# One starting address modulo 512 bytes for the matmul operands, and a gap of 8 columns between two token streams

## The chip, the cores and the metric

The kernel runs on one core of one Trainium2 chip. The metric is the device time of one execution in microseconds (us); lower is better. The kernel before has a median of 1493.14 us over three runs (1492.9 to 1493.96).

## The reference

Two streams of tokens pass through two layers of width 1024: 512 latent tokens and 256 context tokens. Each layer is a token mixer and a ConvFFN, each behind an RMS norm with a modulation (scale, shift, gate) made from a condition vector.

```python
def conv_mixers(h, ...):              # layer 0, both streams
    g_b, g_c, u_a, v_b, gate_b = split(h @ w_in)          # 1024 -> 2560
    y_a = g_b * dwconv3(g_c * u_a)
    u = dwconv31(v_b * sigmoid(gate_b)) + bias
    return concat([y_a, silu(layernorm(u))]) @ w_out      # 1024 -> 1024
def windowed_gqa(h, hc, ...):         # layer 1: 16 heads, 4 key heads, +-128 tokens and all context
    ...
def conv_ffn(h, w_up, conv, w_down):  # both layers; layer 1 for the latent tokens only
    a, g = split(dwconv3(h @ w_up))                       # 1024 -> 2 x 2816
    return (silu(g) * a) @ w_down                         # 2816 -> 1024
```

The output is the latent stream after a last RMS norm, in float32.

## The kernel before

Channels lie on the 128 partitions and tokens along the free dimension. One tile holds 128 channels of both streams side by side: columns 0 to 511 are latent tokens, then a gap of zeros, then 256 context columns from column `C0`; the whole width is `T` (770 columns, lines 27 and 28). The gap lets one elementwise instruction, and one three-tap convolution, run over both streams at once.

**Products.** Float32 precision comes from three products of split operands. Weights are loaded by a DMA into `wraw` and split into `whi` and `wlo` (ACT L158, DVE L159); activations are split the same way into pairs `h` (high and low), `gh` and `gl`, `oh` and `ol`. For each 128-channel tile k of the contraction, `mm3` (L176 to L178) issues three matmuls: `wlo` with the high part, `whi` with the low part, `whi` with the high part. The weights are the stationary operand, 128 columns of 4 bytes, so 512 bytes of each partition; the tokens are the moving operand. `wide_gemm` (L187) runs the 512 latent columns over all k first, then the 256 context columns: 24 matmuls of 512 columns and 24 of 256 for one output tile with eight k.

```python
        for k in range(len(rhs)) if ks is None else ks:                       # L183
            xh, xl = rhs[k]
            self.mm3(out, w, k, xh[:, lo:hi], xl[:, lo:hi], k == first, k == last)
```

**Stages in order.** (1) First norm and the first part of the modulation, with three output tiles of `w_in` alongside. (2) The rest of the 20 tiles of `w_in`; DVE runs the 31-tap convolution between (L577, `tap`), and 12 half pieces of the modulation go between as small products (L225). (3) `w_out`, 8 tiles, half of them held until the LayerNorm of the wide convolution is through. (4) FFN of layer 0: 44 up tiles with eight k, then 22 k for each of 8 down tiles in five groups (`up`, `down`). (5) Keys (2 tiles), queries (8 tiles) and values of layer 1. (6) Attention, with transposes and products in float32, and the output projection `w_o` in two halves of 256 tokens. (7) FFN of layer 1 for 512 latent tokens: the first 6 up tiles and the last group of down products in two halves of 256 columns, the others 512 columns wide. (8) The last norm, transposed out.

**Order.** The order on each engine comes from the program and from a planner that lists the instructions with a time model; `issue_after` ties a few steps to others. Every weight load is issued from SP's queue into a ring of three `wraw` tiles; `whi` and `wlo` are rings of three in the pool `wts`, and some weights go to spare tiles of the current phase instead.

**Where tiles lie.** Each pool is a stretch of SBUF. Constants, `x`, weights and temporaries lie at the low end, the tiles of a phase after them; the pools called `right` (`act` with the tiles `h`, `core`, and the phase `ffn1`) end at the top. A tile takes a multiple of 32 bytes in each partition. At the bottom lies a scratch of 16384 bytes for DMA descriptors, which this kernel's DMAs (all from SP) don't use. A tile that reuses the room of an older one waits for the older one's last use.

```python
C0 = SEQ + 2                                                                  # L27
T = C0 + CTX                                                                  # L28
    self.x = [self.cst.tile([P, T], F32, name=f"x{k}") for k in range(KT)]    # L118
    hi, lo = into or (self.wts.tile([P, 1024], F32R, name=t, tag=t, bufs=3) for t in ("whi", "wlo"))   # L165
    return [tuple(self.act.tile([P, n], F32R, name="h", ...) for c in "hl") for k in range(KT)]        # L328
    gh = self.ph.tile([P, width], F32R, name="gh", tag=f"gh{j}")              # L604
```

From these sizes the starts modulo 512 bytes follow. A tile of `T` columns is 3080 bytes, takes 3104, and 3104 = 6 x 512 + 32, so of a row of such tiles each starts 32 bytes further on. The weights' rings start at 224. The 16 tiles `h` of layer 0 (high and low of k = 0, then of k = 1, and so on) start at 480, 0, 32, 64, ... up to 448, so the high part of k = 4 starts at 224. A context column block starts 514 x 4 = 2056 = 4 x 512 + 8 bytes into its tile. In the FFN of layer 1 the tiles `h` are 512 columns wide and all start at 352; `gh` and `gl` all start at 480, and the weights of the down products lie at 480 (spare tiles of the phase, two of each three) or at 224 (the ring). `oh` and `ol` start at 352.

Of the kernel before, what the change touches and what calls it, by code (L numbers as in the profile page):

```python
# [26 lines left out]
C0 = SEQ + 2  # L27
T = C0 + CTX  # L28
FF = 2816
# [28 lines left out]
class Kern:  # L58
# [38 lines left out]
    def gap(self, slot):  # L97
        """Zeros between the two streams of an accumulator that is as wide as both."""
        self.nc.vector.memset(slot[:, SEQ:C0], 0.0)

# [10 lines left out]
    def setup(self):  # L111
# [5 lines left out]
        self.par = self.cst.tile([P, NPAR], F32, name="par")  # L117
# [12 lines left out]
        # modulation: [ch, layer, chunk*8 + tile, condition]  # L130
        self.mod = self.cst.tile([P, 2, 48, 2], F32, name="mod")
        # gain * (1 + scale): [ch, norm, tile, condition]
# [8 lines left out]
    def turn(self, slots):  # L141
        """A new round of accumulators."""
        self.slots, self.slot_i = slots, 0

    def taken(self):
        """An accumulator, out of the round, and the others in the order in which they come up."""
        s = self.slot()
        i = self.slot_i % len(self.slots)
        return s, (self.slots[i:] + self.slots[:i])[:-1]
# [6 lines left out]
    def split(self, src, hi, lo):  # L156
        """hi + lo = src, each of at most twelve significant bits."""
# [3 lines left out]
    def weights(self, dram, n=1024, into=None):  # L161
        """The two parts of a stretch of weights."""
# [6 lines left out]
    def spare(self, i, n=1024, tags=("whi", "wlo")):  # L169
        """Room for more weights in the current phase."""  # L170
# [9 lines left out]
    def gemm(self, out, w, rhs, lo, hi, ks=None, ends=None):  # L180
        """out = w.T @ rhs[lo:hi], or the tiles ks of a sum from the first to the last of ends."""
# [9 lines left out]
    def places(self, segs):  # L191
        """New accumulators for stretches of tokens."""
# [6 lines left out]
    def side_by_side(self, slots, rhs, segs):  # L199
        """Products with the weights at hand, all of them with one tile of rhs before the next."""  # L200
# [13 lines left out]
    def mod_piece(self, l, lo, hi, at, dram, acc, tr, room):  # L214
        """512 columns of w_mod, as four column tiles of the array: two feature tiles in each half of lo..hi; in two steps."""
# [25 lines left out]
    def mod_rows(self, l, j0, n, conds):  # L241
        """n feature tiles from j0 of w_mod transposed, to be done one after the other."""
# [31 lines left out]
    def square_in(self, k, lo, hi, sq=None):  # L274
        """Adds x[k]**2 to the sum over channel tiles."""
# [9 lines left out]
    def inverse(self, ss, chunks, ones2, comp, eng):  # L285
        """1 / sqrt(mean + EPS) of each token, tokens on the partitions; one column for each chunk of them."""
# [7 lines left out]
        # a first guess from the exponent's bits, then Newton's steps  # L294
# [8 lines left out]
    def rstd(self, ss, segs, ones2, slot, eng=None, pool=None, project=None):  # L303
        """1 / sqrt(mean + EPS) for each token, the same in every partition, in PSUM."""
# [21 lines left out]

    def new_h(self, n=T):
        return [tuple(self.act.tile([P, n], F32R, name="h", tag=f"h{c}{k}") for c in "hl") for k in range(KT)]  # L328

    def mod_in(self, h, k, r, n, l, shift, segs):  # L330
        """h[k] = rmsnorm(x[k]) * gain + shift, in two parts."""
# [5 lines left out]
        for s0, s1 in segs:  # L337
# [4 lines left out]
            if k < 2:  # L342
                # the shorter way for the tiles that are waited for
# [20 lines left out]
    def conv3(self, acc, u, w, n):  # L364
        """acc = three taps over u (zero between the streams)."""
# [5 lines left out]
    def project(self, w, n, rhs, segs, l, chunk, ms=range(KT), lead=0, late=0, few=(), room={}):  # L371
        """x += gate * (w.T @ rhs). The late feature tiles take the last tokens in a second step, with the weights they
        still hold; those in the lead wait for the last of rhs side by side. The last of the steps stops
        after each number in few of its tiles. room: where weights go."""
# [36 lines left out]
    def start(self, ph):  # L411
        """First norm and modulation; value and gate of the wide convolution's first channels alongside."""
# [35 lines left out]
    def layer0_input(self, h, sl):  # L448
        """Value and gate of the wide convolution's channels, then the narrow convolution; the wide one's taps between."""
# [16 lines left out]
    def gates(self):  # L466
        """The rest of the modulation, half a piece at a time."""
# [8 lines left out]
    def layer0_output(self, y):  # L476
        """Output projection: the narrow convolution's channels while the wide one's norm is under way, then the others."""
# [30 lines left out]
    def tokens_in_turn(self, segs, project, norm, first, early=1, room=()):  # L508
        """Projects one stretch of tokens after the other; the norm of each hides behind the next products."""
        self.pre = [self.weights(w) for w in first[:early]]  # L510
        next(project)
        self.h = self.new_h(segs[-1][1])
# [9 lines left out]
    def spread(self, seg, project=None):  # L522
        """1 / rms of a stretch of tokens in SBUF, a step of other work alongside."""
# [8 lines left out]
    def tap(self, n):  # L532
        """n taps of the wide convolution, channel tiles in turn so that none waits for the one before it."""
        for _ in range(n):
# [3 lines left out]
            # the first two tiles first, and those that have the most to go  # L538
# [8 lines left out]
    def tile_in(self, m, h, segs):  # L547
        """One tile of the input projection, its weights made ready one tile ahead."""
# [8 lines left out]
    def glu(self, j, v, g):  # L557
# [3 lines left out]
        if j == 3:  # L561
            # the table of functions that comes next
            with self.tc.issue_after(sigmoid.ins):
                nc.scalar.activation(self.tmp.tile([P, 1], F32, name="z", tag="z", bufs=4), self.ones2[:, 0:1], AF.Silu)
        ub = self.ph.tile([P, CB_W], F32, name="ub", tag=f"gh{4 + j}")
# [4 lines left out]
        # the wide convolution, a tap at a time  # L570
        w = self.p("convb").rearrange("p (j k) -> p j k", k=CB_TAPS)[:, j, :]
        acc = self.ph.tile([P, CB_W], F32, name="cacc", tag=f"gl{4 + j}")[:, :CB_N]
# [8 lines left out]
        if j == 1:  # L581
            self.cs = self.ph.tile([P, CB_N], F32, name="cs", tag="cs")
# [20 lines left out]
    def pair(self, j, src, n, width):  # L603
        gh = self.ph.tile([P, width], F32R, name="gh", tag=f"gh{j}")  # L604
        gl = self.ph.tile([P, width], F32R, name="gl", tag=f"gl{j}")
# [3 lines left out]
    def conv_norm(self, slot, out):  # L609
        """LayerNorm over channels, then SiLU."""  # L610
# [24 lines left out]
        def finish(j, i):  # L635
            (lo, hi), (d0, d1) = segs[i], (LAT, CTXS)[i]
            if i == 0:
                out[4 + j] = tuple(
                    self.ph.tile([P, T], F32R, name=t, tag=tag)
# [421 lines left out]
```

## Time and profile before

| | us |
|---|---|
| median of three runs | 1493.14 |
| lowest, highest | 1492.9, 1493.96 |
| span of the profiled execution | 1491.3 |
| PE busy | 1456.9 (98%) |
| DVE busy | 1023.7 (69%) |
| ACT busy | 594.9 (40%) |
| POOL busy | 47.1 (3%) |

No time outside the trace is given for the profiled execution itself; its span lies 1.8 us under the median, and a change is reckoned on the span and carried over to the median. Matmuls overlap: in the trace one of 512 columns is 0.39 us long with a modelled end, while the next one starts 0.23 us after it. So what a matmul costs is read from the distance of two starts, not from its duration. PEld is the weight load that runs beside the matmul before.

### The profile page before, as it was taken

What the parts mean: (1) busy time and instruction counts of PE and PEld (TensorE: products, weight loads), DVE (VectorE), ACT (ScalarE), POOL (GpSimd) and SP (SyncE); (2) the same over time, 40 slices, a digit from 0 to 9 for tenths busy, and PEclk for the clock granted to TensorE, in tenths of its full rate; (3) what the DMA queues carried; (4) which work ended last, traced back from release to release, by engine and by line L of the source; (5) the groups of instructions that cost most, each with busy time, mean ns of one, the idle gap of its engine ahead of it and who ended that gap; (6) DMA issues with size and microseconds to landing.
All of it is one profiled execution on the core that took longest, in us unless ns stands there. A gap on an engine that the chain in (4) does not pass through costs nothing.

```text
span 1491.3 us, 21938 instructions
## 1 busy us (share of the span) xinstructions
PE 1456.9 (98%) x8786; PEld 1236.1 (83%) x8786; DVE 1023.7 (69%) x1635; ACT 594.9 (40%) x983; POOL 47.1 (3%) x186
## 2 busy tenths in 40 slices
PE   5999999999999999999999999999999999999998
PEld 4888888888888888888888878868799888888887
DVE  6699998679877756456434679786676854655455
ACT  5421224463213223123122376686664442424235
POOL 0000001110000000000000010110000000000000
PEclk9999999999999999999999999999999999999999
DMA  9314434034543532342211324011154333233222
GB/s 374 113 61 170 156 114 136 30 105 148 163 131 124 184 99 85 108 133 82 88 44 44 98 79 141 10 43 51 45 176 162 94 105 104 79 108 95 93 77 75
DMA packets 52709, 161.23 MB, mean 108 GB/s; under 512 B 6400, under 2 KB 6528, under 8 KB 52480
## 3 DMA queue, kind: packets, MB, share of 16 engines
q1 hardware_dynamic: 52608, 159.84, 32.6%
q8 instruction: 68, 1.11, 0.3%
q14 instruction: 33, 0.27, 0.1%
HBM read 155.10 MB, written 2.10 MB: 105 GB/s over the span
## 4 chain that ended last, share of the span: by engine, by line
PE 91%; DVE 3%; DMA 2%; ACT 2%; issue 1%; POOL 0%; DVEq 0%; ACTq 0%
PE slot L176 22%; PE slot L177 21%; PE slot L178 21%; PE av L177 3%; PE av L176 3%; PE av L178 3%; PE av L928 2%; PE pt L918 2%; PE s L899 2%; PE pt L176 2%; PE pt L177 2%; PE pt L178 2%; PE slot L225 1%; PE slot L211 1%; PE slot L207 1%; PE slot L208 1%
## 5 line engine op out<-in xcount | busy, mean ns | idle before, releaser
L176 PE MATMUL slot<-h,wlo 128*128 128x512 f32 (+1 forms) x1192 | 414.9, 350 | 2.2 <-DVE ub L569 1.1
L178 PE MATMUL slot<-h,whi 128*128 128x512 f32 (+1 forms) x1192 | 415.5, 349 | 0.0
L177 PE MATMUL slot<-h,whi 128*128 128x512 f32 (+1 forms) x1192 | 415.1, 349 | 0.2 <-DVE h L349 0.2
L158 ACT CAST whi<-wraw 128x1024 fp32r<-128x1024 f32 (+2 forms) x215 | 191.8, 900 | 210.6 <-PE slot L178 110.4
L176 PEld LDWEIGHTS slot<-h,wlo 128*128 128x128 f32 x1192 | 224.1, 188 | 37.3 <-issue 1.8
L177 PEld LDWEIGHTS slot<-h,whi 128*128 128x128 f32 x1192 | 225.1, 189 | 31.7 <-DVE h L349 0.5
L178 PEld LDWEIGHTS slot<-h,whi 128*128 128x128 f32 x1192 | 225.1, 189 | 30.5
L159 DVE TENSOR_TENSOR wlo<-wraw,whi 128x1024 fp32r<-128x1024 f32 (+2 forms) x215 | 222.0, 1038 | 23.8 <-ACT whi L158 23.3
L369 DVE SCALAR_TENSOR_TENSOR cf<-slot,par,cf 128x769 f32<-128x769 f32 (+1 forms) x132 | 122.0, 927 | 146.6 <-ACT cf L367 146.1
L176 PE MATMUL slot<-gh,wlo 128*128 128x512 f32 (+1 forms) x459 | 157.5, 344 | 0.4 <-DVE x L359 0.4
L367 ACT ACTIVATE cf<-slot,par 128x770 f32<-128x770 f32 (+1 forms) x66 | 55.0, 834 | 256.7 <-PE slot L178 244.1
L177 PE MATMUL slot<-gl,whi 128*128 128x512 f32 (+1 forms) x459 | 156.7, 342 | 0.0
L178 PE MATMUL slot<-gh,whi 128*128 128x512 f32 (+1 forms) x459 | 156.2, 341 | 0.0
L359 DVE SCALAR_TENSOR_TENSOR x<-slot,mod,x 128x256 f32<-128x256 f32 (+1 forms) x139 | 81.8, 617 | 81.0 <-PE slot L178 80.8
L577 DVE SCALAR_TENSOR_TENSOR cacc<-ub,par,cacc 128x783 f32<-128x783 f32 x120 | 118.3, 1035 | 0.2
L253 DVE CUSTOM_DVE_ANT_0 junk<-wmod,cb 128x1024 bf16<-128x1024 f32 x80 | 97.5, 1219 | 9.4 <-DMA wmod<-in_wmt 5.8
L176 PEld LDWEIGHTS slot<-gh,wlo 128*128 128x128 f32 x459 | 86.4, 189 | 12.3 <-issue 0.7
L177 PEld LDWEIGHTS slot<-gl,whi 128*128 128x128 f32 x459 | 86.6, 189 | 10.9 <-issue 0.2
L178 PEld LDWEIGHTS slot<-gh,whi 128*128 128x128 f32 x459 | 86.7, 189 | 10.5
L906 DVE CUSTOM_DVE_ANT_0 sm<-s,mask,nsink 128x640 f32<-128x640 f32 (+1 forms) x58 | 46.8, 819 | 16.0 <-PE pt L918 12.4
L703 ACT ACTIVATE sgf<-cf 128x770 f32<-128x770 f32 (+1 forms) x44 | 32.6, 741 | 61.3 <-DVE cf L369 61.1
L909 ACT ACTIVATE sm<-sm,nm 128x513 f32<-128x513 f32 (+1 forms) x64 | 50.0, 785 | 10.3 <-DVE nm L906 5.4
(244 smaller groups left out, 2247.0 us busy)
## 6 DMA issues: line engine op xcount, KB each, us to landing
wraw<-in_w_up SPq DMA_DIRECT2D x88, 512.0 KB, 3.4
wmod<-in_wmt SPq DMA_DIRECT2D x56, 512.0 KB, 3.9
wmod<-in_wm SPq DMA_DIRECT2D x40, 512.0 KB, 4.9
wraw<-in_w_down SPq DMA_DIRECT2D x48, 256.0 KB, 2.7
wraw<-in_w_in SPq DMA_DIRECT2D x20, 512.0 KB, 4.1
wraw<-in_w_down SPq DMA_DIRECT2D x32, 320.0 KB, 3.0
wraw<-in_w_o SPq DMA_DIRECT2D x16, 512.0 KB, 3.3
wraw<-in_w_out SPq DMA_DIRECT2D x16, 256.0 KB, 3.5
```

What stands on the lines that cost most here:

```text
L158: self.act_mark = self.nc.scalar.copy(hi, src)
L159: self.mark = self.nc.vector.tensor_tensor(lo, src, hi.bitcast(F32), op=ALU.subtract)
L176: mm(out, lo, xh, start=first, stop=False)
L177: mm(out, hi, xl, start=False, stop=False)
L178: self.product = mm(out, hi, xh, start=False, stop=last)
L253: nc.vector.tensor_tensor_reduce(junk, w, self.cb[:, c, :], 1.0, 0.0, ALU.mult, ALU.add, col)
L359: self.nc.vector.scalar_tensor_tensor(self.x[k][:, lo:hi], acc, self.mod[:, l, chunk * 8 + k, c:c + 1], self.x[k][:, lo:hi], op0=ALU.mult, ...
L367: nc.scalar.activation(acc[:, :n], u[:, :n], AF.Copy, scale=w[:, 1:2])
L369: nc.vector.scalar_tensor_tensor(acc[:, o], u[:, i], w[:, j:j + 1], acc[:, o], op0=ALU.mult, op1=ALU.add)
L577: self.tapped = nc.vector.scalar_tensor_tensor(acc, ub[:, t:t + CB_N], w[:, t:t + 1], acc, op0=ALU.mult, op1=ALU.add)
L906: scored = nc.vector.tensor_tensor_reduce(sm[:, :n], s[:, SEQ - nl:SEQ + CTX], mk, -SCALE, nsink[:, hd:hd + 1], ALU.add, ALU.min, nm)
L909: self.scored = scored, nc.scalar.activation(sm[:, :n + 1], sm[:, :n + 1], AF.Exp, scale=-1.0, bias=nm, accum_out=z)
```

## The change

It alters where tiles lie, and the width of the gap. Nothing is added to or taken from the list of instructions. The widths `TW` (896 columns, 3584 = 7 x 512 bytes) and the rounding to 128 columns make every tile of a phase a multiple of 512 bytes; `par`, `sink`, `nsink` and `nm` get filling so that the pools themselves begin at the same address modulo 512 as those at the top; the DMA scratch shrinks from its 16384 bytes to 1024. The gap of 8 columns makes `T` 776: a context block starts 520 x 4 = 2080 = 4 x 512 + 32 bytes into its tile. Comments and docstrings, which the change drops as well, are left out here.

```diff
-C0 = SEQ + 2
+C0 = SEQ + 8
 T = C0 + CTX
+TW = 896
...
-        self.par = self.cst.tile([P, NPAR], F32, name="par")
+        self.par = self.cst.tile([P, NPAR + 64], F32, name="par")[:, :NPAR]
...
-    def new_h(self, n=T):
+    def new_h(self, n=TW):
...
-        self.h = self.new_h(segs[-1][1])
+        self.h = self.new_h(-(-segs[-1][1] // P) * P)
...
-        ub = self.ph.tile([P, CB_W], F32, name="ub", tag=f"gh{4 + j}")
+        ub = self.ph.tile([P, TW], F32, name="ub", tag=f"gh{4 + j}")[:, :CB_W]
...
-        acc = self.ph.tile([P, CB_W], F32, name="cacc", tag=f"gl{4 + j}")[:, :CB_N]
+        acc = self.ph.tile([P, TW], F32, name="cacc", tag=f"gl{4 + j}")[:, :CB_N]
...
-            self.cs = self.ph.tile([P, CB_N], F32, name="cs", tag="cs")
+            self.cs = self.ph.tile([P, TW], F32, name="cs", tag="cs")[:, :CB_N]
...
-        gh = self.ph.tile([P, width], F32R, name="gh", tag=f"gh{j}")
-        gl = self.ph.tile([P, width], F32R, name="gl", tag=f"gl{j}")
+        gh = self.ph.tile([P, -(-width // P) * P], F32R, name="gh", tag=f"gh{j}")
+        gl = self.ph.tile([P, -(-width // P) * P], F32R, name="gl", tag=f"gl{j}")
...
-                    self.ph.tile([P, T], F32R, name=t, tag=tag)
+                    self.ph.tile([P, TW], F32R, name=t, tag=tag)
...
-        room[6] = partial(self.spare, i, n, ("gh", "gl")) if l == 0 else partial(self.spare, 2)
+        room[6] = partial(self.spare, i, TW if l == 0 else n, ("gh", "gl")) if l == 0 else partial(self.spare, 2)
...
-        sink = self.ph.tile([P, NH], F32, name="sink")
+        sink = self.ph.tile([P, P], F32, name="sink")[:, :NH]
...
-        nsink = self.ph.tile([P, NH], F32, name="nsink")
+        nsink = self.ph.tile([P, P], F32, name="nsink")[:, :NH]
...
-            sm = self.core.tile([P, 642], F32, name="sm", tag=f"sm{i % 10}")
-        nm, z = (self.tmp.tile([P, 1], F32, name=t, tag=t, bufs=4) for t in ("nm", "z"))
+            sm = self.core.tile([P, 768], F32, name="sm", tag=f"sm{i % 10}")
+        nm, z = (self.tmp.tile([P, w], F32, name=t, tag=t, bufs=4)[:, :1] for t, w in (("nm", 32), ("z", 1)))
...
-    nc = bacc.Bacc("TRN2", target_bir_lowering=False, num_devices=1)
+    nc = bacc.Bacc("TRN2", target_bir_lowering=False, num_devices=1, dynamic_dma_scratch_size=1024)
```

With these sizes the rings `whi` and `wlo`, the tiles `h`, `gh`, `gl`, `oh`, `ol`, the keys and the queries all start at 480 modulo 512. A context block starts 32 bytes on, at 0. Some operands of float32 matmuls (`x`, `ident`, the rows `sm` in the temporaries' pool) still lie elsewhere.

## Rows read from the trace of the kernel before

**Rows 1.** The page: busy time by engine, and the granted clock in 40 slices.
```profile
PE 1456.9 (98%) x8786; PEld 1236.1 (83%) x8786; DVE 1023.7 (69%) x1635; ACT 594.9 (40%) x983; POOL 47.1 (3%) x186
...
PEclk9999999999999999999999999999999999999999
```

**Rows 2.** Windows: stretch, its us, busy by engine (x instructions), clock, DMA share, GB/s.
```profile
0.00:28.00 28.00, 11.30 (x132) 7.51 (x132) 17.51 (x41) 15.77 (x21) 0.20 (x4) 1.00 0.95 362
58.00:221.00 163.00, 161.86 (x1227) 138.54 (x1227) 155.28 (x169) 39.55 (x54) 1.89 (x1) 1.00 0.35 123
221.00:296.00 75.00, 73.52 (x403) 61.38 (x402) 55.23 (x100) 30.88 (x60) 10.77 (x39) 1.00 0.23 78
296.00:857.00 561.00, 559.55 (x3181) 488.93 (x3181) 356.56 (x498) 168.39 (x220) 8.38 (x26) 1.00 0.35 109
857.00:946.00 89.00, 85.78 (x472) 73.68 (x471) 75.08 (x133) 56.48 (x102) 8.39 (x21) 0.98 0.32 96
946.00:1087.00 141.00, 138.54 (x1021) 103.58 (x1019) 103.76 (x292) 103.36 (x240) 10.41 (x58) 1.00 0.12 39
1149.00:1479.00 330.00, 329.68 (x1538) 272.13 (x1537) 197.38 (x282) 121.35 (x186) 0.00 (x0) 1.00 0.29 91
```

**Rows 3.** Waits of PE, the longest: us in total, times, longest.
```profile
PE slot L290 <- DVE ss L283: 16.4, 3, 14.1
```

**Rows 4.** Timeline of PE, one up tile of layer 0's FFN: start, us, instruction.
```profile
543.90 0.39 PE L176 MATMUL slot<-h,wlo 128*128 128x512 f32 x1
...
544.59 0.40 PE L176 MATMUL slot<-h,wlo 128*128 128x512 f32 x1
...
545.30 0.39 PE L176 MATMUL slot<-h,wlo 128*128 128x512 f32 x1
...
546.69 0.39 PE L176 MATMUL slot<-h,wlo 128*128 128x512 f32 x1
...
547.38 0.40 PE L176 MATMUL slot<-h,wlo 128*128 128x512 f32 x1
...
549.47 0.28 PE L176 MATMUL slot<-h,wlo 128*128 128x256 f32 x1
...
551.98 0.28 PE L176 MATMUL slot<-h,wlo 128*128 128x256 f32 x1
...
552.35 0.39 PE L176 MATMUL slot<-h,wlo 128*128 128x512 f32 x1
```

**Rows 5.** The same, FFN of layer 1: first up product of a run, first down product after.
```profile
1257.99 0.40 PE L176 MATMUL av<-h,wlo 128*128 128x512 f32 x1
...
1300.69 0.39 PE L176 MATMUL av<-gh,wlo 128*128 128x512 f32 x1
```

**Rows 6.** The same: first down product of two runs, each with the next up product.
```profile
1183.98 0.39 PE L176 MATMUL pt<-gh,wlo 128*128 128x512 f32 x1
...
1189.43 0.40 PE L176 MATMUL av<-h,wlo 128*128 128x512 f32 x1
...
1378.49 0.39 PE L176 MATMUL pt<-gh,wlo 128*128 128x512 f32 x1
...
1405.71 0.40 PE L176 MATMUL pt<-h,wlo 128*128 128x512 f32 x1
```

**Rows 7.** The same, 256 columns in layer 1: output projection, and the last down group.
```profile
1097.60 0.28 PE L176 MATMUL av<-oh,wlo 128*128 128x256 f32 x1
...
1108.99 0.28 PE L207 MATMUL slot<-h,wlo 128*128 128x256 f32 x1
...
1450.50 0.28 PE L176 MATMUL pt<-gh,wlo 128*128 128x256 f32 x1
...
1474.96 0.50 PE L290 MATMUL slot<-ones,ss 128*128 128x2 f32 x4
```

**Rows 8.** Groups of DVE from 58 to 221 us: busy, mean ns, idle before.
```profile
L577 DVE SCALAR_TENSOR_TENSOR cacc<-ub,par,cacc 128x783 f32<-128x783 f32 x117 | 115.2, 1035 | 0.2
L369 DVE SCALAR_TENSOR_TENSOR acca<-z,par,acca 128x769 f32<-128x769 f32 x8 | 8.1, 1013 | 0.0
```

## The prediction

> **What bounds the kernel now.** I read the page first: PE is busy 98% of the span, every slice of the granted clock shows 9 (the 2.4 GHz level), and no other engine is above 69% [rows 1]. Then the windows: from 296 to 857 us (layer 0's FFN) and from 1149 to 1479 us (layer 1's FFN) PE is idle for under 2 us in all, while DVE is busy 64% and 60% [rows 2]. The list of waits holds one large entry, the first norm's sum at the start [rows 3]. So 60% of the span is a chain of matmuls that wait for nobody, and the time there is their number times the distance of two starts. Two stages differ: from 58 to 221 us DVE is busy 155.28 of 163 us, and from 946 to 1087 us DVE and ACT are both busy 73 to 74% with chains of softmax between [rows 2].
>
> Next the timeline, for the distance of starts. In layer 0's FFN one up tile takes 24 matmuls of 512 columns from 543.90 to 549.47, 232 ns each, and 24 of 256 columns until 552.35, 120.0 ns each [rows 4]. At the clock of these windows 512 columns are 213.3 ns and 256 are 106.7, so each has some 13 to 19 ns on top. Does this extra depend on where operands start? The code says where they do, and three places in the trace compare.
> - Layer 1's FFN, up products: tokens at 352 modulo 512, weights at 224, one relation for the whole run. 183 matmuls go from 1257.99 to 1300.69: 233.3 ns each [rows 5].
> - Same stage, same shape, down products: tokens at 480, weights at 480 or 224, equal or half of 512 apart. 120 matmuls go from 1378.49 to 1405.71: 226.8 ns. A run of 24 whose weights lie in spare tiles, all at 480, takes 5.45 us: 227.1 ns [rows 6].
> - Layer 0's up tile, where each k has its own start: the distances differ within one tile. The three matmuls of k = 1 (tokens at 32 and 64, weights at 224) take 0.71 us, from 544.59 to 545.30; the three of k = 4 (tokens at 224 and 256) take 0.69, from 546.69 to 547.38 [rows 4].
>
> So a 512-column matmul costs about 227 ns where tokens and weights start alike, and 232 to 233 where they don't. The change makes them alike everywhere; that is its whole lever, since it neither adds nor removes an instruction.
>
> **The change part by part.** Matmuls of 512 columns, by the code (24 for a tile of eight k): w_in 20 tiles, 480; w_out 192; layer 0's up 44 tiles, 1056, and down 528; keys and queries 240; layer 1's up, without the six tiles done in halves, 912; down without the last group, 408.
> - Layer 0 (2256 of them): 232 to 227, that is 5.0 ns each, -11.3 us.
> - Keys and queries (240): tokens lie as in layer 0, so the same 5.0 ns: -1.2.
> - Layer 1's up (912): 233.3 to 227.0, 6.3 ns each: -5.7.
> - Layer 1's down (408): alike already, 0.
> Sum -18.2 us, if PE sets the pace wherever they stand. Where it doesn't, I take back:
> - The start. 72 of the 480 run among waits for the norm and the first loads; until 28 us PE is idle for 16.7 [rows 2]. +0.4.
> - 58 to 221 us. 408 matmuls would save 2.0 us, but DVE has 7.7 us of idle time there, and its taps, 117 of 1035 ns, are the stage's other chain [rows 2, 8]. What is late next is the LayerNorm behind the last tap. I take half back, +1.0; none and all are the ends.
> - 221 to 296 us. 192 matmuls, 1.0 us, beside the LayerNorm's chain of ACT, DVE and POOL; PE is idle 1.5 us there [rows 2]. Half back, +0.5.
>
> Matmuls of 256 columns:
> - Context blocks (2304: 480 + 192 + 1056 + 528 + 48 for the keys). They start 8 bytes past a multiple of 32 now and at a multiple after; tokens then start 32 bytes past the weights, a relation that no row shows for 256 columns. Bounds: below, 96 matmuls of the output projection, 128 apart, at 11.39 us, 118.6 ns each [rows 7]; above, the last three of the up tile, 0.37 us, 123.3 ns each [rows 4]. That is -3.1 to +7.6 us. I take 120.0 as now, 0: the 204 matmuls of the last down group, equal or half of 512 apart, take 24.46 us, 119.9 ns [rows 7], so at 256 columns an equal start gains nothing over today's mixture.
> - Halves in layer 1 that lie 128 apart now and alike after (192 of the output projection outside attention, 288 of the first up tiles): 118.6 to 119.9, +0.6. In attention PE isn't the pace, so nothing.
>
> Elementwise work over both streams becomes 776 wide: 6/770 of, say, 1013 ns [rows 8] is 8 ns an instruction, and DVE has room in both FFNs (it is what would be late if that cover were gone; 132 such taps are 1 us). The eight loads of x carry 24 bytes more in each partition, 25 KB together, 0.07 us at the 362 GB/s of the first window [rows 2]; it lies on the start's path: +0.1. The smaller DMA scratch costs nothing: no DMA uses it. Wider tiles put a new phase's tiles over other old ones, whose last use they wait for, and the planner may list a few instructions otherwise. The trace can't price that; what PE idles beside the first norm's wait is 1491.3 - 1456.9 - 16.4 = 18 us in the whole span [rows 1, 3], and I see no reason for a sign: 0, with 2 us either way.
>
> Sum: -18.2 + 0.4 + 1.0 + 0.5 + 0.6 + 0.1 = -15.6 us. The profiled span of 1491.3 becomes 1475.7; the median stands 1.8 us above the span, so 1477.5.
>
> **The rivals.**
> 1. *The start doesn't matter.* Up and down products differ in more than addresses: an up tile is followed by three-tap convolutions on ACT and DVE, a down tile by one short gate. If that made the 6 ns, nothing changes: 1493.1. Against it: within one up tile of layer 0, with the same company, k = 1 and k = 4 differ by 0.02 us [rows 4]; and its mean, 232, is neither of layer 1's two. The rounding of the starts to 10 ns leaves some doubt. The Trainium skill speaks for this rival: its page "TensorE: Matmul & The Clock Gate" (Part 2, Step-by-step) says the engine has two independent read ports into SBUF, one for the streaming operand and one for weights; by that, addresses of the two could not matter and the sum would be 0. The rows of the two runs, 233.3 against 226.8, speak against it. Chance 0.06.
> 2. *An equal start is the clash.* A weight load of 512 bytes runs beside each matmul, and tiles that all start alike could collide most. Then the costliest mixture seen, 0.71 us for three or 236.7 ns, holds everywhere: 4.7 ns over 232 on 2496 matmuls, 3.4 on 912 and 9.7 on 408, together 11.7 + 3.1 + 4.0 = +18.8, which gives 1512. It decides where the mean distance passes today's, 231.8. Against it: the 24 matmuls whose two starts were equal took 227.1 [rows 6]. Only a three-way relation that those lack could bring it. Chance 0.03.
> 3. *The context pays.* The gain at 512 columns comes, but 32 bytes apart is a bad relation at 256 columns: 123.3 ns each takes back 7.6, so 1485. For: the same tile shows it for one k. Against: 24 in a row average 120.0 over many relations [rows 4]. Chance 0.11.
> My forecast has 0.80.
>
> **How the numbers follow.** The predicted time is the forecast's, 1477.5. Its own range takes the ends of the unknown costs: all of the takebacks of the middle stages gone and the context at its lower bound, -15.6 - 1.5 - 3.1 - 2 = -22.2, or 1471; up to the third rival's 1485. That leaves out rivals 1 and 2 with 0.09, and a little of the rest. A measurement can tell about 0.2%, 3 us, from no change. Faster are the forecast and the third rival, 0.91; the same the first, 0.06; slower the second, 0.03.
>
> **What would show it.** Distances of starts: 227 in layer 1's up run instead of 233.3; 5.45 us instead of 5.57 for the 24 wide matmuls of a layer 0 tile; 2.88 us as before for its context. The window of layer 0's FFN should be about 8 us shorter, that of layer 1's FFN 6 us. DVE's share from 58 us on should rise, and the first LayerNorm product may wait for a tap. I am wrong in the mechanism if the up run stays at 233, and wrong in a term if a context block leaves 2.88 us or if PE shows new waits at the borders of phases.

## The result, and the profile after

The kernel after takes 1473.74 us (median of four, 1473.42 to 1474.01) beside 1493.29 us for the kernel before (1492.9 to 1493.96): ratio 0.9866, 95% interval 0.9852 to 0.988, that is -19.6 us where -15.6 was forecast. The profiled span is 1471.8 us beside 1491.3, -19.5. Lines of the kernel after stand one higher than before (L177 is before's L176).

The page of the kernel after, the line that answers to [rows 1]:

```profile
PE 1435.4 (98%) x8786; PEld 1228.8 (83%) x8786; DVE 1024.4 (70%) x1635; ACT 596.9 (41%) x983; POOL 47.8 (3%) x186
```

The count of matmuls and weight loads is the same, and PE is busy 21.5 us less: the matmuls themselves became cheaper. The windows of the kernel after, with columns as in [rows 2]; each stretch runs from the same first matmul to the same last one as the stretch of before that it answers to:

```profile
58.15:218.86 160.71, 159.56 (x1227) 137.26 (x1226) 154.99 (x169) 39.62 (x54) 1.89 (x1) 1.00 0.36 125
218.86:293.21 74.35, 72.38 (x402) 60.70 (x400) 55.46 (x100) 31.04 (x60) 10.82 (x39) 1.00 0.24 79
293.21:843.15 549.94, 548.48 (x3182) 483.64 (x3181) 356.67 (x497) 169.20 (x220) 8.63 (x26) 1.00 0.35 111
843.15:931.33 88.18, 84.92 (x472) 73.65 (x471) 75.40 (x135) 56.73 (x102) 8.54 (x22) 0.98 0.33 97
931.33:1072.85 141.52, 138.90 (x1022) 103.78 (x1020) 104.12 (x292) 103.48 (x241) 10.37 (x58) 1.00 0.12 39
1135.14:1459.35 324.21, 323.70 (x1537) 271.82 (x1536) 197.37 (x282) 121.78 (x186) 0.00 (x0) 1.00 0.30 93
```

Between the same matmuls, layer 0's FFN went from 560.99 us before to 549.94, -11.1; layer 1's from 329.79 to 324.21, -5.6; the mixer's stage from 163.32 to 160.71, -2.6. `w_out` (74.65 to 74.35), keys and queries (89.0 to 88.19) and attention (141.31 to 141.51) hardly moved. The granted clock stays where it was, 1.00 in all but one stage, the 2.4 GHz level.

Next the timeline of PE in the kernel after. Four lines are the up tile of layer 0 of [rows 4]: its first wide matmul, its sixth, its first context matmul and the next tile's first. Then come the first matmul of layer 1's up run and the one after it, the same for a down run, and the same for the last group's halves.

```profile
536.15 0.39 PE L177 MATMUL slot<-h,wlo 128*128 128x512 f32 x1
...
537.30 0.39 PE L179 MATMUL slot<-h,whi 128*128 128x512 f32 x1
...
541.61 0.28 PE L177 MATMUL slot<-h,wlo 128*128 128x256 f32 x1
...
544.41 0.39 PE L177 MATMUL slot<-h,wlo 128*128 128x512 f32 x1
...
1242.48 0.39 PE L177 MATMUL av<-h,wlo 128*128 128x512 f32 x1
...
1283.96 0.39 PE L177 MATMUL av<-gh,wlo 128*128 128x512 f32 x1
...
1360.12 0.39 PE L177 MATMUL pt<-gh,wlo 128*128 128x512 f32 x1
...
1387.32 0.39 PE L177 MATMUL pt<-h,wlo 128*128 128x512 f32 x1
...
1430.84 0.28 PE L177 MATMUL pt<-gh,wlo 128*128 128x256 f32 x1
...
1455.31 0.17 PE L291 MATMUL slot<-ones,ss 128*128 128x2 f32 x1
```

The 24 wide matmuls take 5.46 us, 227.5 ns each (232 before); the first five of them take 1.15 us, 230 ns each, and the other 19 take 4.31, 226.8 each. The 24 of the context take 2.80 us, 116.7 ns each (120.0 before), which the forecast did not have. Layer 1's up run [rows 5] follows: 183 matmuls in 41.48 us, 226.7 ns each, where it was 233.3; its down run of 120 [rows 6] takes 27.20 us, 226.7, as before (226.8). The last group's 204 halves [rows 7] take 24.47 us, 119.9, as before.

Summed over every matmul of a kind, each distance to the next start in after less the same one in before (the 8786 stand in the same order):

| matmuls | count | us |
|---|---|---|
| context blocks, 256 wide | 2304 | -7.2 |
| start, wide | 72 | -0.1 |
| mixer's stage, wide | 417 | -1.3 |
| `w_out`, wide | 183 | +0.2 |
| layer 0's FFN, wide | 1584 | -6.0 |
| keys, queries | 240 | -1.0 |
| layer 1's up, wide | 912 | -6.0 |
| layer 1's down, wide | 408 | +0.3 |
| layer 1's 256 wide: halves (912), values (144), scores (192) | 1248 | +0.9 |
| all others | | +0.2 |

Together -20.0 us by the unrounded terms. The span lost 19.5, because the first matmul starts 0.37 us later than before and the end takes 0.15 us longer.

Last, the waits of PE in the kernel after (total, times, longest), as in [rows 3]:

```profile
PE slot L291 <- DVE ss L284: 17.1, 4, 14.5
...
PE slot L622 <- ACT r L634: 1.0, 1, 1.0
```

The first norm's sum stays the one large wait. The second line, the LayerNorm's first product behind ACT's `r`, was 0.5 us before; that half microsecond is about what `w_out` lost of its gain. And the three-tap convolution on DVE in the mixer's stage, as in [rows 8]:

```profile
L370 DVE SCALAR_TENSOR_TENSOR acca<-z,par,acca 128x775 f32<-128x775 f32 x8 | 8.2, 1024 | 0.0
```

The six more columns cost it 11 ns an instruction (1013 to 1024), about the 8 ns reckoned.

### The profile page after: what moved, and what is told of

The parts are those of the page before. It is cut to its first block, busy times and chain, and to the rows that moved or that the text cites. A ratio compares the mean times of both kernels' runs of the same rounds, so it can differ in the third digit from the quotient of the medians.

```text
span 1471.8 us, 21937 instructions
## 1 busy us (share of the span) xinstructions
PE 1435.4 (98%) x8786; PEld 1228.8 (83%) x8786; DVE 1024.4 (70%) x1635; ACT 596.9 (41%) x983; POOL 47.8 (3%) x186
## 4 chain that ended last, share of the span: by engine, by line
PE 91%; DVE 4%; ACT 2%; issue 1%; DMA 1%; POOL 1%; DVEq 0%; SPq 0%; ACTq 0%; POOLq 0%
PE slot L177 21%; PE slot L178 21%; PE slot L179 21%; PE av L178 3%; PE av L177 3%; PE av L179 3%; PE av L929 2%; PE pt L919 2%; PE s L900 2%; PE pt L179 2%; PE pt L178 2%; PE pt L177 2%; PE slot L226 1%; PE slot L212 1%; PE slot L208 1%
## 5 line engine op out<-in xcount | busy, mean ns | idle before, releaser
L177 PE MATMUL slot<-h,wlo 128*128 128x512 f32 (+1 forms) x1192 | 410.5, 346 | 2.2 <-DVE ub L570 1.2
L178 PE MATMUL slot<-h,whi 128*128 128x512 f32 (+1 forms) x1192 | 410.8, 345 | 0.2 <-DVE h L350 0.2
L179 PE MATMUL slot<-h,whi 128*128 128x512 f32 (+1 forms) x1192 | 410.8, 345 | 0.0
L177 PEld LDWEIGHTS slot<-h,wlo 128*128 128x128 f32 x1192 | 223.5, 188 | 34.3 <-issue 2.0
L370 DVE SCALAR_TENSOR_TENSOR cf<-slot,par,cf 128x775 f32<-128x775 f32 (+1 forms) x132 | 122.7, 932 | 136.5 <-ACT cf L368 136.0
L177 PE MATMUL slot<-gh,wlo 128*128 128x512 f32 (+1 forms) x459 | 156.7, 342 | 0.7 <-DVE x L360 0.4
L368 ACT ACTIVATE cf<-slot,par 128x776 f32<-128x776 f32 (+1 forms) x66 | 55.3, 837 | 243.1 <-PE slot L179 230.7
L578 DVE SCALAR_TENSOR_TENSOR cacc<-ub,par,cacc 128x783 f32<-128x783 f32 x120 | 118.6, 1040 | 0.2
L177 PEld LDWEIGHTS slot<-gh,wlo 128*128 128x128 f32 x459 | 86.1, 188 | 12.0 <-DVE wlo L160 0.7
L704 ACT ACTIVATE sgf<-cf 128x776 f32<-128x776 f32 (+1 forms) x44 | 32.7, 744 | 60.9 <-DVE cf L370 60.4
```

The source lines that it names most:

```text
L177: mm(out, lo, xh, start=first, stop=False)
L178: mm(out, hi, xl, start=False, stop=False)
L179: self.product = mm(out, hi, xh, start=False, stop=last)
L368: nc.scalar.activation(acc[:, :n], u[:, :n], AF.Copy, scale=w[:, 1:2])
L370: nc.vector.scalar_tensor_tensor(acc[:, o], u[:, i], w[:, j:j + 1], acc[:, o], op0=ALU.mult, op1=ALU.add)
L578: self.tapped = nc.vector.scalar_tensor_tensor(acc, ub[:, t:t + CB_N], w[:, t:t + 1], acc, op0=ALU.mult, op1=ALU.add)
```

## The experiments

Two questions: is it the place of the operands that made the gain, and why did 256 columns, forecast at nothing, give more than a third of it? In what follows d is the start of the tokens less the start of the weights, in bytes of a partition. `C0` puts a context block at d = 8 in before's gap of 2 columns (plus the row's own start), 32 in after's gap of 8. Each version ran beside the kernel before, whose median was 1492.72 to 1493.59 us in those sessions; the ratios are taken against it.

**1. Matmuls alone, d swept.** The kernel's pattern of three matmuls over eight k, from tiles that lie still, 48 matmuls for each d; nothing else runs beside.

```python
for n, b, d in CONFIGS:                  # columns, base, distance in bytes
    b, d = b // 4, d // 4
    for _ in range(2):
        for k in range(KT):
            lo, hi = (t[:, b + k * P:b + (k + 1) * P] for t in w)
            xh, xl = (t[:, b + d:b + d + n] for t in h[k])
            mm(s, lo, xh, ...); mm(s, hi, xl, ...); mm(s, hi, xh, ...)
```

> A kernel of matmuls alone: the model is left out, and its output is not the reference's. Groups of 48 matmuls in the same pattern of three (wlo with high, whi with low, whi with high; eight k) run with all weights at one start and all tokens d bytes past it modulo 512; d goes from 0 to 480 by 32, then 8, 16, 24, 512, 544, 640 and 768, for 512 and for 256 columns; then d = 0, 32, 128 again with both starts moved by 64 and by 128 bytes. Theory A (the difference of the two starts sets the distance): 512 columns 227 ns at 0 and 256, 233 at 128, up to 236 elsewhere; 256 columns 120 at 0 and 256, 117 at 32, 118.6 at 128; the same at 512, 544, 640, 768 as at 0, 32, 128, 256, and the same when both are moved. Rival B (the address of each operand alone, or a tile that is a multiple of 512 bytes): no curve over d with the same shape after both are moved; moving both changes the values as much as moving one. Rival C (starts play no part without other engines at work): all 512-column groups within 1 ns.

Its timeline of PE: the first matmul at d = 0, at d = 32 and at d = 64 (512 columns), at d = 256 and after it, then 256 columns at d = 8, at 16 and after it.

```profile
55.90 0.39 PE L59 MATMUL slot<-h,wlo 128*128 128x512 f32 x1
...
66.78 0.40 PE L59 MATMUL slot<-h,wlo 128*128 128x512 f32 x1
...
77.98 0.40 PE L59 MATMUL slot<-h,wlo 128*128 128x512 f32 x1
...
145.01 0.40 PE L59 MATMUL slot<-h,wlo 128*128 128x512 f32 x1
...
155.90 0.40 PE L59 MATMUL slot<-h,wlo 128*128 128x512 f32 x1
...
402.86 0.28 PE L59 MATMUL slot<-h,wlo 128*128 128x256 f32 x1
...
408.46 0.28 PE L59 MATMUL slot<-h,wlo 128*128 128x256 f32 x1
...
413.90 0.28 PE L59 MATMUL slot<-h,wlo 128*128 128x256 f32 x1
```

48 matmuls take 10.88 us at d = 0 (226.7 ns), 11.20 at 32 (233.3), 10.89 at 256 (226.8). By distance, the mean from start to start inside a group, in ns:

```
d            0     8    16    24    32    64    96   128   160   192   224   256
512 cols 226.7 233.3 231.7 233.2 233.4 229.1 233.6 233.4 234.1 233.2 233.2 226.8
256 cols 119.9 116.7 113.3 120.0 117.9 117.9 119.8 118.6 118.6 117.8 118.3
```

Moving both starts by 64 or 128 bytes changed no value of 512 columns by more than 1.2 ns and none of 256 by more than 0.2; the 1.2 ns, at d = 128, come as well when the same starts run a second time behind another group (232.2). So the place matters with no other engine at work: the first rival falls. At 512 columns the best of these is an equal start, and the pattern repeats after 256 bytes. At 256 columns an equal start is among the worst. One value missed what was expected: 32 bytes gave 117.9 ns, not the 117 (116.8 in the kernel after).

**2. The weights' ring moved away.** The kernel after, with two fillers that put the rings `whi` and `wlo` 128 bytes below the tokens (160 for the context); all else stays as in after.

```diff
+        self.cst.tile([P, 96], F32, name="pada")
+        self.tmp.tile([P, 32], F32, name="padb", bufs=1)
```

> The changed kernel with its rings of weights alone moved down by 128 bytes modulo 512, everything else where it was: tokens start 128 bytes past the weights for 2892 of the 3816 wide matmuls, and 160 past them for 1734 of the context blocks; every tile is still a multiple of 512 bytes. Theory A: 233 ns in the up run of layer 1's FFN (227 in the changed kernel), 5.6 us for the 24 wide matmuls of a layer 0 up tile, +17 us from those; the context blocks go from 116.8 to somewhere between 117 and 123, +0 to +11; in all 1490 to 1502 us. Rival B (multiples of 512 bytes among the tokens and among the weights are what counts, not the one against the other): 227 ns, 1474 us.

1488.58 us, ratio 0.9968 (0.9957 to 0.9979): 14.8 us of the 19.6 are gone. Its timeline of PE: the same up tile of layer 0, then layer 1's up run.

```profile
542.07 0.40 PE L179 MATMUL slot<-h,wlo 128*128 128x512 f32 x1
...
547.67 0.28 PE L179 MATMUL slot<-h,wlo 128*128 128x256 f32 x1
...
550.52 0.39 PE L179 MATMUL slot<-h,wlo 128*128 128x512 f32 x1
...
1253.90 0.40 PE L179 MATMUL av<-h,wlo 128*128 128x512 f32 x1
...
1296.43 0.39 PE L179 MATMUL av<-gh,wlo 128*128 128x512 f32 x1
```

5.60 us for 24 wide ones, 233.3 ns each, 2.85 for the context, 118.8, and 42.53 for the 183, 232.4: the values of experiment 1 at d = 128 and 160 (233.4 and 118.6), the last one by 1 ns less. Tokens that lie alike among themselves are not enough; it is the distance from the weights that pays. The time came a little under the expected stretch, since not every matmul takes its weights from the ring.

**3. The two parts of the change apart.** First after with the old gap, then before with the new one.

```diff
-C0 = SEQ + 8
+C0 = SEQ + 2
```

> The changed kernel with the gap of 2 columns back: all starts alike, but the context blocks start 8 bytes past the weights, not 32. Theory A (the gap's 32 bytes gave the context's 3.2 ns): wide matmuls stay at 227.7, the context tile of 24 goes from 2.80 back to about 2.88 us, +7 us: 1479 to 1483. Rival (aligned tiles gave the context its gain, and 8 bytes do as well as 32): 1473 to 1475.

1479.7 us (1479.42 to 1480.53), ratio 0.991 (0.9897 to 0.9924). The up tile in its timeline of PE:

```profile
539.56 0.40 PE L177 MATMUL slot<-h,wlo 128*128 128x512 f32 x1
...
545.03 0.28 PE L177 MATMUL slot<-h,wlo 128*128 128x256 f32 x1
...
547.91 0.40 PE L177 MATMUL slot<-h,wlo 128*128 128x512 f32 x1
```

The wide ones keep their gain (5.47 us), the context is back at 2.88 us, 120.0 ns.

```diff
-C0 = SEQ + 2
+C0 = SEQ + 8
```

> The kernel before with a gap of 8 columns and nothing else: its tiles take the same 3104 bytes, so all tiles stay where they were, and only the context blocks start at multiples of 32 bytes. Theory A: wide matmuls stay at 232 ns; the context blocks run through all the multiples of 32 and lie at 118 to 120, -4.6 to 0 us: 1488 to 1493. Rival (a start at a multiple of 32 is all that the context needed): 116.8 for all, -7.4 us: 1486.

1487.37 us (1487.06 to 1487.85), ratio 0.996 (0.9947 to 0.9972). The context of the same tile in its timeline of PE:

```profile
546.14 0.28 PE L176 MATMUL slot<-h,wlo 128*128 128x256 f32 x1
...
548.96 0.39 PE L176 MATMUL slot<-h,wlo 128*128 128x512 f32 x1
```

2.82 us, 117.5 ns each, with the wide ones near where they were (231.5 in the mean of all). This came under the stretch that the first theory gave and over its rival's figure: the gap pays even where the rows' starts are scattered. The two parts add up: the starts alone -13.5 us (1493.2 to 1479.7), the gap alone -5.8, together -19.3 where the change brought -19.6.

**4. A finer sweep.** The same matmuls alone, 256 columns in steps of 4 bytes, 512 in steps of 8, over one period.

```python
CONFIGS += [(256, 0, d) for d in range(0, 256, 4)]
CONFIGS += [(512, 0, d) for d in range(0, 256, 8)]
```

> The kernel of matmuls alone again (the model is left out), in finer steps: 256 columns with tokens 0 to 252 bytes past the weights in steps of 4, then 512 columns in steps of 8. Theory A (a curve over the difference modulo 256 bytes, finer than 32): 256 columns 119.9 at 0, 116.7 at 8, 113.3 at 16, 120.0 at 24, 117.9 at 32, as in the first such run, with other low places between; 512 columns lowest at 0, 226.7, 229 at 64, and 231 to 234 elsewhere. Rival E (the few low values at 8 and 16 hang on what ran before them): 8 and 16 give other values here, 118 to 120.

```
d            0     4     8    12    16    20    24    28    32    64   112   136   192
256 cols 119.8 123.0 116.9 116.7 113.3 122.1 120.1 115.6 116.7 117.8 114.2 122.7 113.8
d            0    64   104   120   248
512 cols 227.8 228.9 230.0 239.9 230.1
```

At 256 columns the pace goes from 113.3 to 123.0 ns with no order by distance that I can read; 16 bytes repeated its 113.3 and 8 its 117, which spoke against the rival E. But 32 gave 116.7 where experiment 1 had 117.9, and 192 gave 113.8 beside 117.8. At 512 an equal start stays the best and d = 120 is the worst, 239.9.

**5. The gap that this sweep calls best.** After, with the context at d = 16.

```diff
-C0 = SEQ + 8
+C0 = SEQ + 4
```

> The changed kernel with a gap of 4 columns: same tiles and addresses, and only the context blocks start 16 bytes past the weights, not 32. Theory A with the value of the kernel of matmuls alone, 113.3 ns: the context blocks save 3.5 ns on 2304 matmuls, -8 us: 1465.5 us. Rival E (that value doesn't carry over, as 116.7 ns at 8 bytes became 119.9 in the kernel with the gap of 2): 117 to 120 ns, 1474 to 1481 us.

1476.2 us (1475.55 to 1477.36), ratio 0.9889 (0.9873 to 0.9906): 2.5 us slower than after, where the pace of the sweep would have given 1465.5. The context of the up tile in its timeline of PE:

```profile
542.88 0.28 PE L177 MATMUL slot<-h,wlo 128*128 128x256 f32 x1
...
545.73 0.40 PE L177 MATMUL slot<-h,wlo 128*128 128x512 f32 x1
```

2.85 us, 118.7 ns, not 113.3. The rival E, that this value doesn't carry over to the kernel, holds.

**6. Is it the base?** The weights of the microkernel start elsewhere modulo 512 than the kernel's, so both starts were moved together, over five bases.

```python
CONFIGS += [(256, b, d) for b in (0, 32, 64, 96, 352) for d in (0, 8, 16, 32, 64, 112, 192, 240)]
```

> The kernel of matmuls alone (the model is left out): weights start at 128, 160, 192, 224 and 480 modulo 512, and for each of these the tokens start 0, 8, 16, 32, 64, 112, 192 and 240 bytes past them with 256 columns, and 0, 64, 120 and 128 past them with 512. Theory A (the difference alone counts): five times the same, 113.3 ns at 16, 116.8 at 8, 120 at 0; then the 118.4 ns that the gap of 4 gave in the kernel comes from something else in the kernel. Theory F (the common start counts too, modulo 64): weights at 160, 224 and 480, which are 32 modulo 64, give 118 to 119 at 16 and 120 at 8, as the kernel did with its weights at 480, and 128 and 192 give 113.3 and 116.8.

All five bases agree with one another at each d, within 0.1 ns. But d = 16 gives 116.7 ns here, 8 gives 120.0, and 64 gives 113.4, where experiment 1 had 113.3, 116.7 and 117.9. Its timeline of PE, 256 columns: the first matmul at d = 8, at d = 16 and after it (5.76 and 5.60 us for 48).

```profile
61.56 0.28 PE L55 MATMUL slot<-h,wlo 128*128 128x256 f32 x1
...
67.32 0.28 PE L55 MATMUL slot<-h,wlo 128*128 128x256 f32 x1
...
72.92 0.28 PE L55 MATMUL slot<-h,wlo 128*128 128x256 f32 x1
```

The base is out. The code and, at the first base, the addresses of experiments 1 and 6 are the same; what differs is the order of the groups. For d = 8 the group before had another d (224 modulo 256 there, 0 here). For 16 and 64 the group before had the same d in both, 8 and 32, but ran at another pace itself: 116.7 and 117.9 ns there, 120.0 and 116.7 here. So the pace of a group does not follow from its d and the d before it alone; it hangs on the chain of groups before.

**7. In turns, as in the kernel.** 24 matmuls of 512 columns at d = 0, then 24 of 256 columns at d, and so on, each d twice: the order of a tile with its context.

```python
for d in range(0, 256, 4):
    CONFIGS += [(512, 0, 0), (256, 0, d)] * 2
```

> The kernel of matmuls alone (the model is left out), now in the kernel's own order: 24 matmuls of 512 columns with equal starts, then 24 of 256 columns with the tokens d bytes past the weights, twice for each d from 0 to 252 in steps of 4. Theory G (at 256 columns a group keeps one of several paces, and which one it falls into hangs on what ran before): at 0, 8, 16 and 32 this order gives the four kernels' own values, 119.9, 120.0, 118.5 and 116.8 ns, and both rounds of a d agree. Theory H (something else of the kernel, such as what the other engines do, set the kernels' values): 116.8 at 8 or 113.3 at 16 again.

Its timeline of PE: the first context matmul and the next wide one at d = 8, 16, 32 and 112.

```profile
71.32 0.28 PE L55 MATMUL slot<-h,wlo 128*128 128x256 f32 x1
...
74.20 0.40 PE L55 MATMUL slot<-h,wlo 128*128 128x512 f32 x1
...
104.53 0.28 PE L55 MATMUL slot<-h,wlo 128*128 128x256 f32 x1
...
107.38 0.40 PE L55 MATMUL slot<-h,wlo 128*128 128x512 f32 x1
...
171.12 0.28 PE L55 MATMUL slot<-h,wlo 128*128 128x256 f32 x1
...
173.92 0.39 PE L55 MATMUL slot<-h,wlo 128*128 128x512 f32 x1
...
504.34 0.28 PE L55 MATMUL slot<-h,wlo 128*128 128x256 f32 x1
...
507.10 0.39 PE L55 MATMUL slot<-h,wlo 128*128 128x512 f32 x1
```

2.88, 2.85 and 2.80 us for 24, that is 120.0, 118.7 and 116.8 ns: the very values of the kernels with gaps of 2, 4 and 8 columns. Both turns of each d agree. The best is d = 112 with 115.0 ns (a gap of 28 columns), the worst d = 104 with 128.3. The wide groups between, all at d = 0, run at 226.6 to 229.3 ns depending on the group before. Behind the context at d = 32 they run at 227.7, as in the kernel after. There the 40 unbroken groups of 24 of layer 0's FFN show where it goes: the median distances are 230, 236, 228, 232 and 231 ns for the first five matmuls and 227 for each of the other 19. So something is carried into a group from what ran before it. At 512 columns and d = 0 it is gone after a few matmuls; at 256 columns it can set the pace of the whole group. The price of a distance has to be measured in the kernel's own order.

**8. The gap that the turns call best.** After with the context at d = 112; fillers keep the other starts.

```diff
-C0 = SEQ + 8
+C0 = SEQ + 28
...
-        self.par = self.cst.tile([P, NPAR + 64], F32, name="par")[:, :NPAR]
+        self.par = self.cst.tile([P, NPAR + 128], F32, name="par")[:, :NPAR]
...
+        self.tmp.tile([P, 112], F32, name="pad", bufs=1)
```

> The changed kernel with a gap of 28 columns (and filling so that the weights and tokens still start alike): the context blocks start 112 bytes past the weights, the lowest place of the kernel of matmuls in turns, 115.0 ns against 116.8 at 32 bytes. Theory G: 1.8 ns on 2304 matmuls, -4.1 us, less some 0.5 us for elementwise work that is 796 columns wide and not 776: 1469 to 1471 us. Rival (the wider elementwise work on DVE, busy over 95% of the wide convolution's stage, sets the pace there): that stage is no shorter than in the changed kernel, and the whole 1471 to 1475.

1471.07 us (1470.29 to 1472.6), ratio 0.9851 (0.9838 to 0.9864). The context of the up tile in its timeline of PE, and then the window of the mixer's stage:

```profile
540.89 0.28 PE L178 MATMUL slot<-h,wlo 128*128 128x256 f32 x1
...
543.65 0.39 PE L178 MATMUL slot<-h,wlo 128*128 128x512 f32 x1
```

```profile
58.15:218.07 159.92, 158.75 (x1228) 136.87 (x1228) 154.64 (x168) 40.60 (x54) 2.61 (x1) 1.00 0.36 125
```

2.76 us, 115.0 ns, as in the turns. DVE's wider instructions, 20 columns more again, don't hold the mixer's stage back: it is 0.8 us shorter than in after (160.71).

**9. The halves of layer 1 too.** The same, with the tokens of the output projection and of the last down group 112 bytes past the weights.

```diff
-    def pair(self, j, src, n, width):
+    def pair(self, j, src, n, width, off=0):
...
+        gh, gl = gh[:, off:], gl[:, off:]
...
-            g.append(self.pair(f % ng, sg, n, n))
+            g.append(self.pair(f % ng, sg, n, n + l * P, 28 if l and f >= GROUPS[-1][0] else 0))
...
-        o = [tuple(self.core.tile([P, SEQ], F32R, name=f"o{c}{k}") for c in "hl") for k in range(KT)]
+        o = [tuple(self.core.tile([P, SEQ + P], F32R, name=f"o{c}{k}")[:, 28:28 + SEQ] for c in "hl") for k in range(KT)]
```

> The kernel with the gap of 28, and in layer 1 the attention's outputs and the last group of the second FFN start 112 bytes past the weights too: 624 matmuls of 256 columns, of which 432 lie outside attention. Theory G: they go from 119.9 to 114.4 to 115 ns, -2.1 to -2.4 us against the gap of 28 alone: 1467 to 1469 us; the last group's 204 in a row from 24.46 to about 23.4 us. Rival H (layer 1's halves run at 120 for another reason, such as the gates that follow on DVE): no change against the gap of 28.

1468.92 us (1468.31 to 1470.06), ratio 0.9837 (0.9823 to 0.985), the fastest version here, 4.8 us under after and 24.4 under before. Its timeline of PE: the output projection's 96 matmuls, then the last group's 204.

```profile
1079.49 0.28 PE L178 MATMUL av<-oh,wlo 128*128 128x256 f32 x1
...
1090.38 0.28 PE L209 MATMUL slot<-h,wlo 128*128 128x256 f32 x1
...
1427.21 0.28 PE L178 MATMUL pt<-gh,wlo 128*128 128x256 f32 x1
...
1450.37 0.17 PE L292 MATMUL slot<-ones,ss 128*128 128x2 f32 x1
```

10.89 us is 113.4 ns each (118.6 in [rows 7]); 23.16 us is 113.5 (119.9 in after). These runs, longer than the context's 24, come to less than its 115.0 at the same distance; in experiment 4, too, the 48 matmuls at d = 112 took 115.0 ns each in the first half and 113.3 in the second. The rival H falls.

## Why the prediction was right, and where it was not

**Right: the lever.** The distance of starts is what changed; instructions, clock and the large wait are the same. That tokens and weights that start alike cost 227 ns and others 232 to 233 was read from the up and down runs and shown by experiments 1 and 2. *The start doesn't matter* falls with them: the rule of the Trainium skill ("TensorE: Matmul & The Clock Gate", Part 2, Step-by-step) of two independent read ports does not bring equal times, 226.7 against 233.4 ns with nothing but matmuls running. *An equal start is the clash* falls at 512 columns. *The context pays* falls as well: the relation did matter at 256 columns, but the other way.

**Wrong: "I take 120.0 as now, 0".** The context blocks gave -7.2 us, at 116.8 ns, outside the bounds of 118.6 to 123.3. The step took an equal start, 128 bytes apart and a mixture, saw 118.6 to 120, and concluded that nothing is to be had at 256 columns. But the new distance, 32 bytes, stood in no row; the ends were the nearest rows, the upper one three starts rounded to 10 ns, not limits of the mechanism. It alone is more than the miss: without it the sum would have been -12.8 by the measured terms (-20.0 + 7.2), less than the -15.6 forecast. That the total came out near is in part luck: the wide matmuls gave -13.9 where -16.3 had been set down after the take-backs, and a gain that the sum did not have more than made it up.

**Mis-sized: "232 to 227, that is 5.0 ns each".** In layer 0 the wide matmuls fell to 228.0 on average in the FFN, from 231.9 (6.0 us over 1584, 3.8 ns), and to 228.4 from 231.6 in the mixer's stage; the few over 250 ns, which waited, are left out of these means. 227 is the pace of a long run at one distance, and layer 0 has none: each group of wide matmuls comes behind a context group, and its first five take some 22 ns more together than five at 227 would. A group of 24 comes to 227.7 so, the down tiles' groups of 12 to 228.7. Over the FFN's 79 such groups that is 1.7 us, most of the 1.9 that is missing from the 7.9 of 1584 times 5.0. So layer 0 gave -7.3 us where -11.3 less the take-backs of 1.9 had been set down. Layer 1's up, a run without a context, gave -6.0 beside -5.7, and keys and queries -1.0 beside -1.2.

**The take-backs.** The 1.0 us for the taps was not needed: DVE's idle time in the stage fell from 7.7 to 5.7 us and it never came to set the pace. `w_out` did lose the gain of its wide matmuls (+0.2), where I had taken back half; the LayerNorm's wait of 0.5 us more covers most of it. The start gave next to nothing (-0.1 for 72), as the take-back of 0.4 out of 0.4 had it. For 480 halves +0.6 was reckoned, and they cost +0.5, though 144 of them (three of the six first up tiles, weights and tokens both at 352) lay alike before already; with attention's halves, values and scores it is the +0.9 of the table. The output projection outside attention went from 118.6 to 120.0 in 96 of them, 1083.18 to 1094.70 us.

**Signs.** 227 in the up run: 226.7. 5.45 us for the wide 24: 5.46. 2.88 for the context: 2.80, the sign that a term was wrong. Layer 0's FFN 8 us shorter: 11; layer 1's 6: 5.6. DVE's share of the mixer's stage rose, from 155.28 of 163.00 to 154.99 of 160.71, and the LayerNorm's product waits 0.5 us longer.

**Open.** Why a distance costs what it costs, why it repeats after 256 bytes, and what a group hands to the next: no view shows the reads of PE, so that the two reads get in each other's way is a guess. PE here loads new weights for every matmul; whether the start matters with weights that stay, or for another type, was not tried.

## What to carry to other kernels

Where PE is the chain, read the distance between starts for each shape, and compare places that differ only in where operands start: 3% of a matmul hung on it here, with no instruction changed. Price a placement in the kernel's own order of shapes, since a sweep of one shape alone named a gap (4 columns) that was slower than the one at hand, and the sweep in turns named one (28 columns) that was faster. An unmeasured relation has no bounds from its neighbours; leave room for a gain as well as a loss.

## What the runs showed of the hardware that was not expected

- In one and the same order of groups, the cost of a distance repeats after 256 bytes and does not depend on the base: 226.7 ns at 0 and 226.8 at 256, and five bases with the same values at 256 columns.
- The best distance differs by width: 0 for 512 columns (226.7, and up to 239.9 at 120), but not for 256 (119.9 at 0, from 113.3 up to 128.3 elsewhere).
- The pace depends on what ran before: d = 16 at 256 columns ran at 113.3, 116.7 and 118.7 ns in three orders, and was steady within each. At 512 columns and d = 0 only the start of a group shows it: 228 to 236 ns for the first five matmuls, then 227, in the kernel after.
- The Trainium skill ("TensorE: Matmul & The Clock Gate", Back-to-back issue gap) gives N / 2.4 + 2.5 ns as the gap of matmuls in isolation, by which the estimate would be 215.8 for 512 columns and 109.2 for 256, and about 131 ns for N = 512 in streams of a weight load and a matmul in turn. The runs differ from both: the lowest means of a group in these streams, each matmul with new weights, are 226.6 and 113.3.
